# One inference step of a hybrid backbone: TensorE's order in the recurrent layer written out as a table

## The chip, the core and the metric

The kernel runs on one core of a Trainium2 chip. A core has five engines that run side by side, each with its own in-order instruction queue, and that wait for each other through semaphores: TensorE (PE in the profile, matrix products into PSUM; PEld is its weight load), VectorE (DVE), ScalarE (ACT), GpSimd (POOL) and SyncE (SP), whose queue starts most of the DMA transfers. The metric is the device time of one execution in microseconds (us), as a median of several runs. The clock named in the profile is the share of TensorE's full clock that was granted.

## The reference

Two layers run over 640 tokens of 1024 features: 512 latent tokens, which form a grid of 8 rows and 64 columns, and 128 context tokens. Layer 0 mixes tokens by neighbourhood attention, layer 1 by a recurrent unit in both directions; each is followed by a SwiGLU feed-forward layer. The change is in layer 1's mixer:

```
def _rglru_coeffs(xc, w_a, b_a, w_i, b_i, lam):
    r = sigmoid(einsum('btnk,nkj->btnj', xb, w_a) + b_a)     # xb: xc in 8 blocks of 128 features
    i = sigmoid(einsum('btnk,nkj->btnj', xb, w_i) + b_i)
    log_a = -LRU_C * r * softplus(-lam)
    return exp(log_a), sqrt(-expm1(2.0 * log_a)) * (i * xc)

def _lru_mixer(xm, h0, w_in, conv_w, conv_b, w_a, b_a, w_i, b_i, lam, w_out):
    gate, xr = split(xm @ w_in, 2, axis=-1)
    xc = _centred_depthwise_conv(xr, conv_w, conv_b)
    a_f, b_f = _rglru_coeffs(xc, w_a[0], ...)                # forward
    a_b, b_b = _rglru_coeffs(xc, w_a[1], ...)                # backward
    hs_f, hT_f = _linear_scan(a_f, b_f, h0[:, 0], reverse=False)   # h = a_t * h + b_t
    hs_b, hT_b = _linear_scan(a_b, b_b, h0[:, 1], reverse=True)
    y = (hs_f + hs_b) * gelu(gate)
    return y @ w_out, stack([hT_f, hT_b], axis=1)
```

## The kernel before

Everything is held with features on the 128 partitions, so 1024 features are eight tiles (f = 0 to 7, `KT`), and tokens along the free axis. A tile of features is also one block of the gates' weights: the eight tiles of the recurrent layer don't depend on each other until the output projection.

A plain projection of one output tile (`halves`) loads its weights, splits them into a rounded high half `whi` and a remainder `wlo`, and makes two chunks of tokens, here called a (tokens 0 to 384) and b (384 to 640). A chunk is 24 matmuls into one PSUM tile `mm`: for each of eight input tiles high times high, high times low and low times high (`some`, lines 221 to 223). In this stage the raw weights come over SyncE's queue, `whi` a second time by a DMA on GpSimd's queue (line 178), which writes and rounds it, and VectorE subtracts to get `wlo` (line 182). There are three buffers of each. `lru_xr` projects x, the input of the recurrence: in this text x3a and x3b are the two chunks of x's tile 3, and ScalarE copies them into a buffer `xr` (two of them, taken in turn). `lru_gate` projects the gate branch: chunks g3a and g3b, of which ScalarE takes the gelu.

One tile then passes four steps:

- `lru_a`: ScalarE (line 1252) and three steps of VectorE (line 1254) make the convolution `xc`. TensorE makes four gate products `gp` from `xc` (line 1264), two gates in two directions, each of 643 columns in plain 32-bit floats; ScalarE takes a tanh of each (line 1265, a sigmoid by another formula). Two PSUM buffers hold `gp`, so a product waits for the tanh of the one two before it. VectorE multiplies by `xc` (line 1266).
- `lru_b`: VectorE clamps (line 1272), ScalarE takes two exp, two tanh and one square root (lines 1276 to 1278), VectorE multiplies (lines 1279 and 1280). Switching between the functions loads a table on ScalarE (`ACT_TABLE_LOAD` in the profile).
- `lru_c`: VectorE runs four scans (line 1289), GpSimd copies the last states (line 1291), VectorE adds the directions (lines 1296 and 1297).
- `lru_d`: VectorE multiplies by the gelu (line 1301); ScalarE (line 1306) and VectorE (line 1308) split y into its two halves for the output projection.

The loop in `run` works with t = 0 to 9 and makes, for one t, `lru_a` of tile t, the projection of x's tile t + 1, `lru_b` of tile t - 1, `lru_c` of t - 2, the gate projection of t - 2 and `lru_d` of t - 2. This is the order in which the program is written. What stands in each engine's queue is then set by a planner, which orders instructions by its own estimates of durations and may mix the matmuls of several chunks and products. An order can be forced with `pin`, which lets what is issued inside it come only after a given instruction of the same engine; `chunk` takes such pins for single matmuls. Before the loop, x0a, g0a, x1a, x0b and g0b are made. After it, `project_halves` multiplies y by the output weights: three tiles run over the first six tiles of y, and wait for the last two after that.

## Time and profile before

| | us |
|---|---|
| median of 3 runs (1520.92 to 1523.51) | 1522.5 |
| the profiled execution | 1524.38 |
| its span in the trace | 1522.6 |
| TensorE busy | 1491.2 |
| VectorE busy | 1060.8 |
| ScalarE busy | 698.6 |
| the recurrent stage in the span | about 850 to 1025 |

TensorE is busy for 98% of the span. The mean granted clock is 0.991. The stage of the change is about a tenth of the span. In rows of the trace the first number is the start in us from the span's beginning, the second how long the row is busy; then follow line, engine, operation, output and inputs, shape and count; in brackets stands the idle time of the engine just ahead of the row and what ended it. Rows of one engine overlap a little, because an instruction can start before the one ahead of it has drained. A gate product shows as four matmul records, two for each call. Lines are those of the kernel before; behind the change they lie three to six higher (line 1264 becomes 1268, line 1265 becomes 1269).

### The profile page before, as it was taken

To read this page: it belongs to the slowest core of one execution; us is meant where nothing else is said; L and a number is where in the kernel's file an instruction comes from. 1 tells how busy PE (TensorE), PEld (TensorE's weight loads), DVE (VectorE), ACT (ScalarE), POOL (GpSimd) and SP (SyncE) were. 2 spreads that over 40 slices of the span, in tenths; PEclk is the share of its full clock that TensorE was granted. 3 is DMA by queue.
4 is the path that set the end of the run, shared out by engine and by line. 5 is a ranking of instruction groups with operands and counts; after the bars stand their busy time and mean duration, and the time that the engine had idled before them with its cause. 6 is when DMAs were issued, how large, how long until landed. Compare 5 with 4: busy or idle time off the path is not lost. (4 is left out here: it accounts for less than half of the span.)

```text
span 1522.6 us, 26092 instructions
## 1 busy us (share of the span) xinstructions
PE 1491.2 (98%) x10359; PEld 1443.4 (95%) x10359; DVE 1060.8 (70%) x2005; ACT 698.6 (46%) x1268; POOL 256.2 (17%) x276
## 2 busy tenths in 40 slices
PE   8999999899999999999999999999999999999997
PEld 5999999899999999999999987899999999999997
DVE  5778998669899997434443769875965656556555
ACT  4676766754332123312331478863634343425243
POOL 0112131100111110000000114220222322232211
PEclk9999999999999999999999999999999999999999
DMA  9545665335456664222222543325242231323211
GB/s 379 176 136 162 194 192 165 107 141 193 162 189 202 198 205 127 69 84 79 69 62 94 152 135 102 114 96 183 93 128 73 81 110 58 99 68 97 70 56 70
DMA packets 72330, 196.65 MB, mean 129 GB/s; under 512 B 8048, under 2 KB 24592, under 8 KB 72080
## 3 DMA queue, kind: packets, MB, share of 16 engines
q1 hardware_dynamic: 57392, 142.32, 29.0%
q0 software_dynamic: 14240, 51.98, 11.0%
q8 instruction: 81, 1.33, 0.4%
q10 hardware_dynamic: 576, 0.68, 0.1%
q14 instruction: 41, 0.34, 0.1%
HBM read 179.48 MB, written 8.92 MB: 124 GB/s over the span
## 5 line engine op out<-in xcount | busy, mean ns | idle before, releaser
L221 PE MATMUL mm<-big,whi 128*128 128x320 f32 (+3 forms) x1233 | 384.1, 313 | 5.9 <-ACT big L1306 5.3
L222 PE MATMUL mm<-big,whi 128*128 128x320 f32 (+3 forms) x1233 | 384.3, 312 | 0.5 <-DVE big L563 0.3
L223 PE MATMUL mm<-big,wlo 128*128 128x320 f32 (+3 forms) x1233 | 384.6, 313 | 0.0
L221 PEld LDWEIGHTS mm<-big,whi 128*128 128x128 f32 x1233 | 233.3, 190 | 8.3 <-ACT big L1306 6.1
L222 PEld LDWEIGHTS mm<-big,whi 128*128 128x128 f32 x1233 | 233.8, 190 | 3.0 <-DVE big L563 0.9
L223 PEld LDWEIGHTS mm<-big,wlo 128*128 128x128 f32 x1233 | 233.4, 189 | 1.5
L250 DVE SCALAR_TENSOR_TENSOR mprod<-mraw,csb 128x1024 f32<-128x1024 f32 x160 | 194.9, 1218 | 8.5 <-DMA mraw<-in_wm 8.1
L586 DVE SCALAR_TENSOR_TENSOR x<-mm,G,x 128x320 f32<-128x320 f32 (+2 forms) x192 | 78.0, 435 | 83.2 <-PE mm L223 83.1
L180 ACT CAST whi<-raw 128x1024 fp32r<-128x1024 f32 (+1 forms) x71 | 73.9, 1041 | 111.1 <-PE mm L222 65.7
L182 DVE TENSOR_TENSOR wlo<-raw,whi 128x1024 fp32r<-128x1024 f32 (+1 forms) x87 | 105.5, 1212 | 23.6 <-ACT whi L180 14.5
L221 PE MATMUL mm<-big,whx 128*128 128x320 f32 (+3 forms) x348 | 108.5, 312 | 0.0
L223 PE MATMUL mm<-big,wlx 128*128 128x320 f32 (+3 forms) x348 | 108.3, 311 | 0.0
L222 PE MATMUL mm<-big,whx 128*128 128x320 f32 (+3 forms) x348 | 108.2, 311 | 0.0
L246 POOL DMA_DIRECT2D mraw<-in_wm x80 | 43.0, 537 | 365.7 <-DVE mprod L250 274.2
L221 PE MATMUL mx<-big,whi 128*128 128x320 f32 (+3 forms) x287 | 89.6, 312 | 0.0
L223 PE MATMUL mx<-big,wlo 128*128 128x320 f32 (+3 forms) x287 | 89.1, 310 | 0.0
L222 PE MATMUL mx<-big,whi 128*128 128x320 f32 (+3 forms) x287 | 88.9, 310 | 0.0
L180 ACT CAST whx<-raw 128x1024 fp32r<-128x1024 f32 (+1 forms) x40 | 41.1, 1030 | 91.5 <-PE mm L222 51.6
L223 PE MATMUL mx<-big,wlx 128*128 128x320 f32 (+3 forms) x260 | 80.8, 311 | 0.0
L221 PE MATMUL mx<-big,whx 128*128 128x320 f32 (+3 forms) x260 | 80.8, 311 | 0.0
L222 PE MATMUL mx<-big,whx 128*128 128x320 f32 (+3 forms) x260 | 80.4, 309 | 0.0
L1306 ACT CAST whi<-raw 128x1024 fp32r<-128x1024 f32 (+1 forms) x41 | 41.4, 1009 | 70.7 <-PE mm L222 45.1
(347 smaller groups left out, 3716.2 us busy)
## 6 DMA issues: line engine op xcount, KB each, us to landing
raw<-in_gu SPq DMA_DIRECT2D x88, 512.0 KB, 3.6
mraw<-in_wm POOLq DMA_DIRECT2D x80, 512.0 KB, 3.9
raw<-in_dn SPq DMA_DIRECT2D x24, 512.0 KB, 3.5
sw<-in_wm SPq DMA_DIRECT2D x16, 512.0 KB, 10.1
raw<-in_wqk SPq DMA_DIRECT2D x16, 512.0 KB, 4.7
raw<-in_wi SPq DMA_DIRECT2D x16, 512.0 KB, 3.6
whi<-in_wi POOLq DMA_DIRECT2D x16, 512.0 KB, 3.9
raw<-in_dn SPq DMA_DIRECT2D x16, 448.0 KB, 3.3
```

The lines of the kernel that those rows point to most:

```text
L180: nc.scalar.copy(hi, raw)
L182: nc.vector.tensor_tensor(lo, raw, hi.bitcast(F32), ALU.subtract)
L221: nc.tensor.matmul(ps, hi[:, k], xhi[:, k, s], start=(k == 0), stop=False)
L222: nc.tensor.matmul(ps, hi[:, k], xlo[:, k, s], start=False, stop=False)
L223: self.done = nc.tensor.matmul(ps, lo[:, k], xhi[:, k, s], start=False, stop=(k == last)).ins
L246: nc.gpsimd.dma_start(w, self.i["wm"][l * 6 + j - 2, f])
L250: nc.vector.scalar_tensor_tensor(prod, w, 1.0, self.csb[:, s], ALU.mult, ALU.mult, accum_out=out[:, s, f:f + 1])
L586: self.nc.vector.scalar_tensor_tensor(xs, ps[:, a - t0:b - t0], G[:, s, f:f + 1], xs, ALU.mult, ALU.add)
L1306: self.nc.scalar.copy(hi, v)
```

## The change

A table `ORDER` now says which chunks of plain projections belong to each t, in order. `lru_a` gets these chunks as `steps`. Each gate product is pinned behind the last matmul of whatever chunk came before it, and after each product's tanh the next chunk is issued, its first matmul pinned behind that product. Steps that are left over follow behind `lru_a`. The order on TensorE is thus product, whole chunk, product, whole chunk, and so on; a tile has four products and three chunks (two for tile 7), so the fourth product and the next tile's first stand side by side. Nothing is computed in another way.

The chunks are also dealt out otherwise: x runs ahead of its tile as before up to x4, then x5 is spread over t = 3 and 4; of the gate branch, g1 begins at t = 1 (before, at t = 3) and ends at t = 2, g2 and g3 come at t = 3 and 4, g4 is spread over t = 5 and 6. g6 and g7 come behind the last product, as before.

```
+ORDER = ("x1b x2a x2b", "x3a x3b g1a", "x4a x4b g1b", "x5a g2a g2b", "x5b g3a g3b",
+         "x6a x6b g4a", "x7a x7b g4b", "g5a g5b", "g6a g6b", "g7a g7b")

-    def lru_a(self, f, lp):
+    def lru_a(self, f, lp, steps):
...
                 for s0, s1 in ((0, 512), (512, LW)):
-                    nc.tensor.matmul(ps[:, s0:s1], gw[:, w, d], xc[:, s0:s1], start=True, stop=True)
+                    with self.pin(self.done):
+                        gp = nc.tensor.matmul(ps[:, s0:s1], gw[:, w, d], xc[:, s0:s1], start=True, stop=True).ins
                 nc.scalar.activation(tl[:, d], ps[:, 0:LW], AF.Tanh, scale=0.5, bias=self.hb[:, c:c + 1])
+                if steps:
+                    steps.pop(0)(pins={0: gp})
...
+            chunks = {"x1b": x1[1]}
             for t in range(KT + 2):
+                steps = []
+                for chunk in ORDER[t].split():
+                    if chunk not in chunks:
+                        f = int(chunk[1])
+                        pair = self.lru_xr(f, xhi, xlo) if chunk[0] == "x" else gate(f)
+                        chunks.update({chunk[:2] + c: step for c, step in zip("ab", pair)})
+                    steps.append(chunks[chunk])
                 if t < KT:
-                    A[t] = self.lru_a(t, lp)
-                if t + 1 < KT:
-                    for step in self.lru_xr(t + 1, xhi, xlo) if t else x1[1:]:
-                        step()
+                    A[t] = self.lru_a(t, lp, steps)
+                for step in steps:
+                    step()
                 if 0 < t <= KT:
                     B[t - 1] = self.lru_b(t - 1, *A.pop(t - 1))
                 if t > 1:
                     C[t - 2] = self.lru_c(t - 2, *B.pop(t - 2))
-                if t > 2:
-                    for step in gate(t - 2):
-                        step()
                 if t > 1:
                     self.lru_d(t - 2, C.pop(t - 2), G.pop(t - 2), yhi, ylo)
```

The planner still orders ScalarE, VectorE, GpSimd and SyncE, and comes to other orders there too. The queues of all engines are word for word the same up to the first gate product. The first place is TensorE at that product. Before, `mm_9748` is x2a; x1b has been made in full ahead of it, and the first two products stand in the midst of x2a:

```order
L223 MATMUL mm_9748<-big_8886,wlo_9745 128x384
L1264 MATMUL gp_9672<-xc_9665,gw_9663 128x512
L1264 MATMUL gp_9672<-xc_9665,gw_9663 128x131
L1264 MATMUL gp_9676<-xc_9665,gw_9663 128x512
L1264 MATMUL gp_9676<-xc_9665,gw_9663 128x131
L221 MATMUL mm_9748<-big_8886,whi_9744 128x384
L222 MATMUL mm_9748<-big_8887,whi_9744 128x384
```

Now `mm_9636` is g0b and `mm_9682` is x1b:

```order
L226 MATMUL mm_9636<-big_8886,wlo_9520 128x256
L1268 MATMUL gp_9678<-xc_9671,gw_9669 128x512
L1268 MATMUL gp_9678<-xc_9671,gw_9669 128x131
L224 MATMUL mm_9682<-big_8886,whi_9525 128x256
L225 MATMUL mm_9682<-big_8887,whi_9525 128x256
L226 MATMUL mm_9682<-big_8886,wlo_9526 128x256
```

The first product has moved ahead of x1b, and x2a with it behind the second.

The second place is ScalarE around the exp of tile 0. Before, it comes between the third and the fourth tanh of tile 1 (`lt_9724`; `lt_9670` is tile 0, `xr_1598` holds x3):

```order
L1265 ACTIVATE lt_9724<-gp_9733,l_hb_2009 128x643
L1276 ACT_TABLE_LOAD
L1276 ACTIVATE lt_9802<-lt_9670,l_sm_387_2007 128x643 x2
L1277 ACTIVATE lt_9670<-lt_9670,l_sp_386_2005 128x643
L1265 ACTIVATE lt_9724<-gp_9737,l_hb_2009 128x643
L1277 ACTIVATE lt_9670<-lt_9670,l_sp_386_2005 128x643
L1244 COPY xr_1598_9503<-mm_9870 128x16x8
```

Now (tile 0 is `lt_9676`, tile 1 `lt_9797`, and `mm_9864` is g1a):

```order
L1269 ACTIVATE lt_9797<-gp_9860,l_hb_2009 128x643
L1282 ACT_TABLE_LOAD
L1282 ACTIVATE lt_9895<-lt_9676,l_sm_387_2007 128x643 x2
L1283 ACTIVATE lt_9676<-lt_9676,l_sp_386_2005 128x643 x2
L1322 COPY gl_9782<-mm_9864 128x384
L1284 ACT_TABLE_LOAD
L1284 ACTIVATE lt_9676<-lt_9676 128x1286
L1269 ACT_TABLE_LOAD
L1269 ACTIVATE lt_9797<-gp_9890,l_hb_2009 128x643
```

The exp still stands behind the third tanh of tile 1, but that tanh now belongs to a product with g1a behind it, and the square root of tile 0 comes ahead of the fourth.

The third place is VectorE at the same time. Before, with tile 2's convolution `xc_9813`, tile 3's `xc_9920` and the clamps (L1272) of tiles 1 and 2 (`lt_9723`, `lt_9818`) around tile 0's product with the square root (L1279):

```order
L1254 SCALAR_TENSOR_TENSOR xc_9813<-xr_1597_9502,cols_61,xc_9813 128x643 x2
L1272 TENSOR_SCALAR lt_9723<-lt_9723 128x1286
L1266 SCALAR_TENSOR_TENSOR lt_9724<-lt_9724,xc_9718 128x1286
L182 TENSOR_TENSOR wlo_10114<-raw_10111,whi_10113 128x1024
L1279 SCALAR_TENSOR_TENSOR lt_9670<-lt_9802,lt_9670 128x1286
L1254 SCALAR_TENSOR_TENSOR xc_9920<-xr_1598_9503,cols_61,xc_9920 128x643
L1280 TENSOR_TENSOR lt_9671<-lt_9671,lt_9670 128x1286
L1272 TENSOR_SCALAR lt_9818<-lt_9818 128x1286
```

Now (tile 2's convolution is `xc_9912`, tile 3's `xc_10053`, tile 1's clamp `lt_9796`):

```order
L1257 SCALAR_TENSOR_TENSOR xc_9912<-xr_1597_9502,cols_61,xc_9912 128x643 x3
L1278 TENSOR_SCALAR lt_9796<-lt_9796 128x1286
L185 TENSOR_TENSOR wlo_10041<-raw_10038,whi_10040 128x1024
L1285 SCALAR_TENSOR_TENSOR lt_9676<-lt_9895,lt_9676 128x1286
L1272 SCALAR_TENSOR_TENSOR lt_9797<-lt_9797,xc_9791 128x1286
L1286 TENSOR_TENSOR lt_9677<-lt_9677,lt_9676 128x1286
L1257 SCALAR_TENSOR_TENSOR xc_10053<-xr_1598_9503,cols_61,xc_10053 128x643
```

The product of tile 1's second gate (L1266, now L1272) has moved from ahead of tile 0's L1279 to behind it, and the first step of tile 3's convolution from directly behind it to two steps later.

## The prediction

> **What bounds the kernel now.** The page comes first: TensorE is nearly always busy, so the change can only act where TensorE waits or where what it waits for gets later. Behind the page I cut the recurrent stage into windows (columns: busy time of TensorE, its weight loads, VectorE, ScalarE and GpSimd; granted clock; DMA).

> ```profile
> PE 1491.2 (98%) x10359; PEld 1443.4 (95%) x10359; DVE 1060.8 (70%) x2005; ACT 698.6 (46%) x1268; POOL 256.2 (17%) x276
> ```

> ```profile
> 868.90:908.80 39.90, 39.76 (x236) 33.80 (x235) 24.56 (x24) 27.55 (x41) 2.12 (x4) 1.00 0.49 151
> 908.80:945.00 36.20, 33.88 (x199) 29.48 (x197) 35.45 (x44) 33.95 (x45) 20.57 (x10) 1.00 0.39 117
> 945.00:980.00 35.00, 33.05 (x198) 28.76 (x197) 30.62 (x37) 29.45 (x40) 7.49 (x8) 0.99 0.33 102
> 980.00:1024.70 44.70, 42.74 (x261) 39.17 (x260) 36.20 (x43) 29.08 (x39) 13.56 (x7) 0.96 0.22 75
> sum 155.80, PE 149.42 PEld 131.21 DVE 126.83 ACT 120.04 POOL 43.74; mean PE 37.35 PEld 32.80 DVE 31.71 ACT 30.01 POOL 10.94
> ```

> In this stage three engines are close to full. VectorE does 126.8 us, 15.9 us for each of the eight tiles, and is idle 15.3 us up to 908.8 but only 115.9 - 102.3 = 13.6 us in all the rest. TensorE's timeline has four waits worth naming, 5.8 us together:

> ```profile
> 918.48 1.35 PE L1264 MATMUL gp<-xc,gw 128*128 128x512 f32 x4 [1.87 <-ACT lt L1265]
> 932.24 1.35 PE L1264 MATMUL gp<-xc,gw 128*128 128x512 f32 x4 [0.46 <-ACT lt L1265]
> 979.44 4.09 PE L1264 MATMUL gp<-xc,gw 128*128 128x512 f32 x8 [1.86 <-ACT lt L1278]
> 1022.31 0.42 PE L221 MATMUL mm<-big,whi 128*128 128x320 f32 x1 [1.64 <-ACT big L1306]
> ```

> The third is put down to ScalarE, but what ended last is VectorE's third convolution step, which ends at 978.46 + 0.88 = 979.34. One tile earlier the same step ends at 945.14, just ahead of the gate product:

> ```profile
> 944.23 0.91 DVE L1254 SCALAR_TENSOR_TENSOR xc<-xr,cols,xc 128x643 f32<-128x643 f32 x1
> 945.25 2.40 PE L1264 MATMUL gp<-xc,gw 128*128 128x512 f32 x8
> 978.46 0.88 DVE L1254 SCALAR_TENSOR_TENSOR xc<-xr,cols,xc 128x643 f32<-128x643 f32 x1
> ```

> So from the fourth tile on VectorE's queue hands out the tiles, and the stage ends when y of the last two tiles leaves VectorE (the wait at 1022.31). Two of the waits are followed by some 3.4 us at a clock of 0.5 (the windows beside these rows have 0.88, 0.97 and 0.68), 1.7 us lost each time:

> ```profile
> 980.00:982.00 2.00, 2.00 (x5) 1.11 (x4) 2.00 (x2) 1.09 (x4) 0.00 (x0) 0.50 1.04 387
> 982.00:984.00 2.00, 2.00 (x8) 1.18 (x7) 1.97 (x3) 1.19 (x2) 0.00 (x0) 0.77 0.17 70
> 1024.00:1026.00 2.00, 2.00 (x10) 2.00 (x9) 2.00 (x2) 1.49 (x2) 0.00 (x0) 0.50 0.97 373
> ```

> **The change, part by part.** No product and no chunk is added or removed, so TensorE's work is unchanged; I walk the new queues with durations from these rows.

> ```profile
> 855.19 0.42 PE L221 MATMUL mm<-big,whi 128*128 128x384 f32 x1
> 859.49 0.34 PE L221 MATMUL mm<-big,whi 128*128 128x384 f32 x1
> 870.05 0.28 PE L221 MATMUL mm<-big,whi 128*128 128x256 f32 x1
> 872.89 0.34 PE L221 MATMUL mm<-big,whi 128*128 128x384 f32 x1
> 876.29 2.33 PE L1264 MATMUL gp<-xc,gw 128*128 128x512 f32 x8
> 878.37 0.42 PE L221 MATMUL mm<-big,whi 128*128 128x384 f32 x1
> 868.95 1.81 DVE L1254 SCALAR_TENSOR_TENSOR xc<-xr,cols,xc 128x643 f32<-128x643 f32 x2 [4.87 <-ACT xc L1252]
> 871.50 1.23 DVE L182 TENSOR_TENSOR wlo<-raw,whi 128x1024 fp32r<-128x1024 f32 x1 [0.74 <-DMA whi<-in_wi]
> 872.64 0.89 DVE L1254 SCALAR_TENSOR_TENSOR xc<-xr,cols,xc 128x643 f32<-128x643 f32 x1
> ```

> A 384-column chunk (a) takes 859.49 - 855.19 = 4.3 us, a 256-column one (b) 872.89 - 870.05 = 2.84, a gate product (878.37 - 876.29) / 2, with the slow first instruction behind it 1.08 us.

> (1) The first gate product moves from behind x1b and most of x2a to ahead of x1b, so it comes up at 870.05. Its input is complete at 872.64 + 0.89 = 873.5, because VectorE's queue, in the new order too, has the low half of x2's weights between the steps, and those wait for a DMA until 871.5. TensorE waits 3.5 us. Before, x1b was the cover.

> (2) From 873.55 on: four products, x1b, x2a, x2b put the end of tile 0's products at 873.55 + 4.32 + 2.84 + 4.3 + 2.84 = 887.85; three more products with x3a and x3b bring tile 1's third to 898.2. Then ScalarE's queue has: tanh until 899.2, table load, two exp of tile 0, two tanh, a copy of g1a, table load, square root.

> ```profile
> 893.45 1.28 ACT L1276 ACT_TABLE_LOAD   x1
> 894.75 1.74 ACT L1276 ACTIVATE lt<-lt,l_sm 128x643 f32<-128x643 f32 x2
> 908.20 1.73 ACT L1277 ACTIVATE lt<-lt,l_sp 128x643 f32<-128x643 f32 x2
> 915.23 0.46 ACT L1316 COPY gl<-mm 128x384 f32<-128x384 f32 x1
> 901.18 1.28 ACT L1278 ACTIVATE lt<-lt 128x1286 f32<-128x1286 f32 x1
> 902.49 1.50 DVE L1279 SCALAR_TENSOR_TENSOR lt<-lt,lt 128x1286 f32<-128x1286 f32 x1 [1.34 <-ACT lt L1278]
> ```

> That is 899.2 + 1.28 + 1.74 + 1.73 + 0.46 + 1.28 + 1.28 = 907.0, and the step of L1279 ends near 908.5 where it ended at 904.0. The exp starts at 900.5, not 894.75, because g1a and whole chunks now stand between the products of tiles 0 and 1. What has VectorE done by 908.8? In the new order 9 convolution steps, 5 weight halves, 2 clamps (L1272), one L1266, one L1279. Before, it had done 11, 5, 3, 2 and 1 of these, one L1280 and a scan.

> ```profile
> L1254 DVE SCALAR_TENSOR_TENSOR xc<-xr,cols,xc 128x643 f32<-128x643 f32 x24 | 21.2, 883 | 6.1 <-ACT xc L1252 5.9
> L1289 DVE TENSOR_TENSOR_SCAN lt<-lt,cols,lt 128x512 f32<-128x512 f32 x16 | 20.3, 1270 | 0.0
> L1266 DVE SCALAR_TENSOR_TENSOR lt<-lt,xc 128x1286 f32<-128x1286 f32 x8 | 12.0, 1498 | 11.3 <-ACT lt L1265 11.3
> L1280 DVE TENSOR_TENSOR lt<-lt,lt 128x1286 f32<-128x1286 f32 x8 | 12.0, 1494 | 0.0
> L1272 DVE TENSOR_SCALAR lt<-lt 128x1286 f32<-128x1286 f32 x8 | 6.6, 829 | 0.0
> L1301 DVE TENSOR_TENSOR lt<-lt,gl 128x640 f32<-128x640 f32 x8 | 6.5, 819 | 0.9 <-ACT gl L1320 0.9
> L1265 ACT ACTIVATE lt<-gp,l_hb 128x643 f32<-128x643 f32 x32 | 25.1, 791 | 14.2 <-PE gp L1264 13.9
> ```

> The debt is 2 x 0.88 + 0.83 + 1.50 + 1.49 + 1.2 (the scan up to 908.8) = 6.8 us, in front of a stretch in which VectorE has only 13.6 us of idle time.

> (3) From there each tile needs 15.9 us of VectorE, while TensorE's share per tile is 4 x 1.08 + 4.3 + 4.3 + 2.84 = 15.8 us, or 14.3 with one a and two b. TensorE therefore reaches each next gate product first and waits there for the convolution. Walking the queues tile by tile gives waits of about 1.6, 3.0, 4.2, 2.2 and 2.3 us ahead of tiles 3 to 7, with 3.5 at the start, 0.3 at a PSUM buffer of tile 2 and 1.2 at the end: 18.3 us against 5.8. These waits are the same delay seen from TensorE, not added to it.

> (4) ScalarE gets three table loads more (24 in the stage where before has 21), 3 x 1.28 = 3.8 us. Most lies beside the waits for VectorE. What shows is in the last two tiles, where VectorE waits for the tanh and the square root behind them; with y0's cast and the weights of x6 and g6, which are loaded into buffers that open only when an earlier chunk is through, the walk leaves VectorE some 15.6 us idle after 908.8, against 13.6: 2 us more.

> (5) The earlier gelu branches remove one wait, 0.9 us at L1301; it lies in the tail and is inside (4).

> (6) Clock: the 3.5 us wait at the start is longer than the 1.86 and 1.64 us that were followed by half clock; I add 1.7 us for it, since everything in tile 0 follows from it. Its ends are 0 and 1.7. Later waits I cost at nothing, as TensorE has 1.6 to 4.2 us of slack at the next wait; without that cover each costs up to 1.7. [...] Here a gap of 1.86 us was enough, and one of 1.87 us, at 918.48, was followed by windows at 1.00, so the measurement decides: the length alone doesn't. [...]

> Sum: 6.8 + 2 + 1.7 = 10.5 us. Bounds of the first term: 0, if the later idle time swallows it, and 15.3, all the idle time that VectorE had up to 908.8; of the second: -5, if the waits of the old order's tail are avoided, and +8 if each wait of (3) brings half clock. The profiled execution took 1524.4 us, 1.9 above the median of 1522.5; 1524.4 + 10.5 = 1534.9 there, so **1533** as a median, with a range of its own of 1526 to 1541.

> **The rivals.** *A steady alternation removes the waits* (faster). The four waits and both half-clock stretches go, -5.8 - 3.4, and the new start costs 3.5 + 1.7: -4.0, 1518.5. For it speaks that a whole chunk, at least 2.84 us, now covers each tanh (0.79) between products; against it, that the third wait was VectorE's. It decides if VectorE's idle time after 908.8 falls below 13.6 - 6.8 - 4.0 = 2.8 us, so that the convolution of tiles 3 to 7 is ready ahead of its product.

> *VectorE swallows the debt* (no change): the stage still ends with VectorE, whose work is the same 126.8 us; if 6.8 of its 13.6 us go, y ends as before, and the start wait is TensorE's alone: 1522.5.

> *Waits multiply* (slower still). The five waits of (3) each bring half clock, 5 x 1.7 = 8.5 on top: 1541.5. Also GpSimd copies the scans' last columns, and in the new order both copies of tile 0 stand ahead of the DMA of g2's weights; one copy took long while VectorE ran without a break:

> ```profile
> 911.02 12.53 POOL L1291 COPY st<-lt 128x1 f32<-128x1 f32 x1
> ```

> That would start g2's weights up to 4 us later, until VectorE itself stands still for them: part of the 8.5. [...]

> **How the numbers follow.** My forecast gets 0.54, the rivals 0.2, 0.12 and 0.14. A difference under 0.2% (3 us) is about what a measurement here can't tell from none. Faster: 0.2; same: 0.12; slower: 0.54 + 0.14 = 0.68. For eight in ten the range reaches from the fast rival's 1518.5 to just over the slow one's 1541.5: 1518 to 1543.

> **What would show it.** Right: TensorE's first gate product starts near 873.5 behind a wait of some 3.5 us, then 0.5 clock; VectorE has about 18 us done by 908.8; TensorE waits at the first product of tiles 3 to 7, ended by the convolution; the last two casts of y start near 1032 instead of 1021.5; beyond that the kernel runs as before. Wrong: the convolution is ready ahead of those products, VectorE is fuller after 908.8 than 102 of 116 us, or the last y is cast by 1024.

## The result, and the profile after

The changed kernel takes 1538.47 us (median of 4 runs, 1538.13 to 1539.35) where the kernel before takes 1523.01 in runs beside it (1520.92 to 1524.33). The ratio is 1.0101 with a 95% interval of 1.0083 to 1.012, so the change costs 15.5 us, between 12.6 and 18.3. The prediction was 1533 with a range of 1518 to 1543.

The profiled execution took 1538.3 us with a span of 1536.5, 13.9 more than the span before. Its page gives TensorE 1493.2 us busy where before it was 1491.2: the work is the same, and what grew is the time around it. Here are the windows of the recurrent stage in the changed kernel (columns as in the prediction: TensorE, weight loads, VectorE, ScalarE, GpSimd, granted clock, DMA).

```profile
PE 1493.2 (97%) x10359; PEld 1445.6 (94%) x10359; DVE 1062.6 (69%) x2005; ACT 703.1 (46%) x1271; POOL 249.9 (16%) x276
```

```profile
868.90:908.80 39.90, 36.57 (x213) 32.04 (x212) 16.82 (x17) 20.21 (x32) 2.69 (x5) 0.96 0.48 139
908.80:945.00 36.20, 32.48 (x183) 27.72 (x182) 29.18 (x34) 29.42 (x41) 8.27 (x7) 0.95 0.28 89
945.00:980.00 35.00, 30.80 (x177) 26.63 (x176) 32.78 (x37) 31.06 (x40) 6.99 (x7) 1.00 0.41 126
980.00:1024.70 44.70, 40.71 (x258) 36.98 (x257) 32.28 (x35) 37.96 (x48) 7.48 (x6) 1.00 0.23 66
1024.70:1040.00 15.30, 12.27 (x80) 11.48 (x79) 14.94 (x20) 4.85 (x9) 10.98 (x4) 1.00 0.16 52
sum 171.10, PE 152.82 PEld 134.85 DVE 126.00 ACT 123.49 POOL 36.41; mean PE 30.57 PEld 26.97 DVE 25.20 ACT 24.70 POOL 7.28
```

The stage is 171.1 us long instead of 155.8. VectorE does the same work (126.0 against 126.8) with 45.1 us of idle time instead of 29.0, and TensorE is idle 171.1 - 152.8 = 18.3 us where before it was 155.8 - 149.4 = 6.4. This is where TensorE stands, from its timeline:

```profile
875.36 1.35 PE L1268 MATMUL gp<-xc,gw 128*128 128x512 f32 x4 [3.33 <-DVE xc L1257]
922.75 1.32 PE L1268 MATMUL gp<-xc,gw 128*128 128x512 f32 x4 [1.23 <-issue]
941.04 1.90 PE L1268 MATMUL gp<-xc,gw 128*128 128x512 f32 x4 [2.46 <-ACT gl L1326]
959.33 1.10 PE L1268 MATMUL gp<-xc,gw 128*128 128x512 f32 x2 [2.23 <-issue]
977.15 1.32 PE L1268 MATMUL gp<-xc,gw 128*128 128x512 f32 x4 [1.98 <-issue]
994.26 1.32 PE L1268 MATMUL gp<-xc,gw 128*128 128x512 f32 x4 [2.65 <-ACT lt L1283]
1037.90 0.41 PE L224 MATMUL mm<-big,whi 128*128 128x320 f32 x1 [2.48 <-ACT big L1312]
```

One wait is at the start, five are ahead of the first products of tiles 3 to 7, and one is at the end, for y; the seven come to 16.4 us, and the rest of the 18.3 is short pauses. The profile names "issue" or ScalarE for the five, but what ended last is VectorE's third convolution step each time; for tile 7, at 993.28 + 0.88 = 994.16. This piece of VectorE's timeline also shows what held that step back, the low half of g6's weights, which waited for their DMA:

```profile
988.21 1.82 DVE L1257 SCALAR_TENSOR_TENSOR xc<-xr,cols,xc 128x643 f32<-128x643 f32 x2
992.14 1.23 DVE L185 TENSOR_TENSOR wlo<-raw,whi 128x1024 fp32r<-128x1024 f32 x1 [2.11 <-DMA whi<-in_wi]
993.28 0.88 DVE L1257 SCALAR_TENSOR_TENSOR xc<-xr,cols,xc 128x643 f32<-128x643 f32 x1
```

The last row starts 0.09 us before the one ahead of it ends (992.14 + 1.23 = 993.37).

The kernel before has such a wait for weights at the same place, ahead of the last convolution step of its tile 7, and a longer one, so this wait alone does not make the difference:

```profile
977.32 1.23 DVE L182 TENSOR_TENSOR wlo<-raw,whi 128x1024 fp32r<-128x1024 f32 x1 [2.91 <-DMA whi<-in_wi]
```

The stage itself begins 1.8 us later than in the profile of before, though nothing ahead of it was changed. Over all profiles of this study that start moved by up to 4.8 us from kernel to kernel, and single runs of the kernel before lay between 1516.2 and 1527.5. So from here on stages are compared by times counted from the end of tile 0's convolution (873.53 before, 875.30 after). Three marks are used: the end of the convolution of tile 3 and of tile 7, and the start of ScalarE's last cast of y. A mark comes from the one profiled execution of each kernel.

### The profile page after: what moved, and what is told of

The parts are those of the page before. It is cut to its first block, busy times and chain, and to the rows that moved or that the text cites. A ratio compares the mean times of both kernels' runs of the same rounds, so it can differ in the third digit from the quotient of the medians.

```text
span 1536.5 us, 26093 instructions
## 1 busy us (share of the span) xinstructions
PE 1493.2 (97%) x10359; PEld 1445.6 (94%) x10359; DVE 1062.6 (69%) x2005; ACT 703.1 (46%) x1271; POOL 249.9 (16%) x276
## 5 line engine op out<-in xcount | busy, mean ns | idle before, releaser
L224 PEld LDWEIGHTS mm<-big,whi 128*128 128x128 f32 x1233 | 234.5, 191 | 10.6 <-ACT big L1312 6.9
L183 ACT CAST whi<-raw 128x1024 fp32r<-128x1024 f32 (+1 forms) x71 | 73.9, 1042 | 112.1 <-PE mm L225 68.3
L249 POOL DMA_DIRECT2D mraw<-in_wm x80 | 43.1, 538 | 364.6 <-DVE mprod L253 265.4
```

What stands on the lines that cost most here:

```text
L183: nc.scalar.copy(hi, raw)
L224: nc.tensor.matmul(ps, hi[:, k], xhi[:, k, s], start=(k == 0), stop=False)
L249: nc.gpsimd.dma_start(w, self.i["wm"][l * 6 + j - 2, f])
```

## The experiments

In the table, the third column is the median less that of the kernel before in the same comparison; the last three are the marks, in us from the end of tile 0's convolution.

| kernel | what it is | us against before | tile 3 | tile 7 | last y |
|---|---|---|---|---|---|
| before | | | 38.0 | 105.8 | 148.7 |
| after | order fixed, recurrent chunks and gelus sooner | +15.5 | 47.4 | 118.9 | 164.6 |
| e3 | order fixed alone | +17.9 | 48.5 | 124.8 | 169.2 |
| e2 | order fixed, recurrent chunks sooner | +5.5 | 40.1 | 114.3 | 158.6 |
| e6 | recurrent chunks sooner alone | +7.8 | 38.0 | 114.1 | 153.8 |
| e4 | all gelus g1 to g7 sooner alone | +9.2 | 38.0 | 112.1 | 156.4 |
| e1 | after, x1b ahead of the first product | +11.6 | 43.1 | 117.1 | 164.4 |
| e5 | after, last tile's products together | +13.4 | 48.5 | 120.0 | 162.2 |
| e12 | after, each chunk ahead of its product | +13.2 | 38.2 | 119.9 | 163.5 |
| e9 | after, all products of a tile together | +33.2 | 38.0 | 139.1 | 181.3 |
| e10 | e9, gelus late, x1b first | +23.2 | 35.9 | 131.8 | 172.9 |
| e11 | e9, old dealing, x1b first | +47.6 | 53.0 | 152.2 | 193.2 |
| e8 | before, tanh for gelu | -1.9 | 38.1 | 107.5 | 147.4 |
| e7 | after, tanh for gelu | +15.3 | 47.3 | 119.8 | 164.3 |

### The parts of the change: e2, e3, e4, e6

The change does three things at once: it fixes TensorE's order, it deals the chunks of x2 to x4 and x5a to earlier turns, and it deals g1 to g3 and g4a one or two turns sooner. (Counted in turns of the program, x2 to x4 thus do not run ahead "as before" but one turn more; in TensorE's queue before, the planner had already let x2a begin ahead of tile 0's first product.) Four kernels take the parts apart, the third one only roughly: e4 moves every branch from g1 to g7 one turn sooner, while the change leaves g5 to g7 where they were.

e2, the gelu branches late again:

```diff
-ORDER = ("x1b x2a x2b", "x3a x3b g1a", "x4a x4b g1b", "x5a g2a g2b", "x5b g3a g3b",
-         "x6a x6b g4a", "x7a x7b g4b", ...
+ORDER = ("x1b x2a x2b", "x3a x3b", "x4a x4b", "x5a g1a g1b", "x5b g2a g2b",
+         "x6a x6b g3a g3b", "x7a x7b g4a g4b", ...
```

> The changed kernel, but each gelu branch is dealt as late as in the kernel before (g1 among the products of tile 3, g2 of tile 4, and so on); the recurrent chunks and the fixed alternation are kept. Theory (whole chunks among the products of tiles 0 and 1 make the debt, the gelu branches a small part: the copy of g1a, 0.46, and one table load, 1.28, ahead of the first square root): 1538.5 - 1.7 = 1537, with 1535 to 1539. Rival (the earlier gelus carry the loss through ScalarE's table loads and GpSimd's late copies): near the kernel before, 1523 to 1529.

e3, the old dealing in the fixed order:

```diff
+ORDER = ("x1b", "x2a x2b", "x3a x3b", "x4a x4b g1a g1b", "x5a x5b g2a g2b",
+         "x6a x6b g3a g3b", "x7a x7b g4a g4b", ...
```

> The fixed alternation alone: each tile's products are pinned one behind the other with chunks between, but chunks and gelu branches are dealt to the same tiles as in the kernel before, so that only x1b stands among the products of tile 0 (873.5 + 4 x 1.08 + 2.84 = 880.7 instead of 887.9 for their end). Theory (the debt comes from the chunks dealt to tiles 0 and 1): 6.8 of the 15.5 us are given back, 1538.5 - 6.8 = 1532, the start wait and its half clock stay. Rival (the alternation itself, with a product at the head of every tile, makes the loss whatever is dealt): 1537 or more.

e4, on the kernel before:

```diff
-                if t > 2:
-                    for step in gate(t - 2):
+                if 1 < t <= KT:
+                    for step in gate(t - 1):
```

> The kernel before with one edit: the gelu branch of tile t - 1 instead of t - 2 is dealt in turn t; no order of TensorE is fixed. Theory (an earlier gelu by itself saves at most the 0.9 us that VectorE waited for a gelu and costs a table load or two): 1523 within 3. Rival (the earlier gelus carry the loss): 1530 or more.

e6, on the kernel before:

```diff
+EARLY = ("x1b x2a x2b", "x3a x3b", "x4a x4b", "x5a", "x5b", "x6a x6b", "x7a x7b", "", "", "")
...
-                if t + 1 < KT:
-                    for step in self.lru_xr(t + 1, xhi, xlo) if t else x1[1:]:
-                        step()
+                for chunk in EARLY[t].split():
...
```

> The kernel before with the recurrent chunks dealt as early as in the changed kernel (x2 in turn 0, x3 in turn 1 and so on), but no order of TensorE fixed and the gelu branches where they were. Theory from the runs so far (with the order fixed, the earlier recurrent chunks gave back 10.6 us in the stage; without it, VectorE waits only 5.9 us for the convolution's first step, 4.9 of them at the start): 1521 to 1524. Rival (step 2 of the prediction: chunks of x2 and x3 dealt to tiles 0 and 1 hold their products back and make VectorE's debt): 1523.5 + 6.8 = 1530.

Measured: e2 1529.15 (ratio 1.004, 1.0025 to 1.0054), e3 1541.6 (1.0124, 1.01 to 1.0149), e4 1532.83 (1.0065, 1.0046 to 1.0085), e6 1529.22 (1.0049, 1.0031 to 1.0068). All four theories missed in size or in sign; the rivals of e3 and e4 had the number, and that of e2 nearly (it ended at 1529). Together the four give the account. Fixing the order alone costs 17.9 us. In the fixed order, the earlier recurrent chunks give 12.4 of them back (17.9 to 5.5), and the earlier gelus cost 10.0 (5.5 to 15.5). Without a fixed order the earlier recurrent chunks cost 7.8, so they only mend what the fixed order breaks: there a tile's products come at the head of its turn, and with the old dealing the next tile's input is still to be computed behind them (in e3 TensorE waits 2.43, 4.23 and 3.99 us ahead of tiles 1 to 3). The 9.2 us of e4 look like the 10.0, but they do not show that the change's earlier gelus cost as much without a fixed order: e4 moves g5 to g7 too, and its loss lies at the end, where these are missing. (In e6 the rival had the number, 1530, but not the place: tile 3's convolution is not late, tile 7's is.)

A part of these sums is the clock, which was 0.50 behind some of the waits (two stretches of 3.41 us in the changed kernel). From 6 us ahead of the origin to the last y, TensorE was idle for 6.2 us in the kernel before, 18.0 in e3, 11.4 in e2 and 18.3 in the changed kernel; half of its busy time at a clock of 0.50, my estimate of what the half clock cost it, was 1.7, 9.0, 4.4 and 3.4 us. (It is a little high: in the changed kernel matmuls of 256 columns start 0.21 us apart at a clock of 0.50, from 876.98 to 879.97, and 0.12 apart at 1.00 just behind.) So what the earlier recurrent chunks gave back in the fixed order was 6.6 us of waits and 4.6 us of clock, and what the earlier gelus cost was waits.

What e4 and e6 lose shows at one place, TensorE's wait ahead of the next projection (1.64 us in the kernel before). The first row is e4's, from its timeline:

```profile
1030.04 0.63 PE L221 MATMUL mm<-big,whi 128*128 128x320 f32 x1 [6.92 <-ACT big L1306]
```

and this is the same place in e6:

```profile
1025.65 0.63 PE L222 MATMUL mm<-big,whi 128*128 128x320 f32 x1 [7.79 <-ACT big L1307]
```

In both a stretch at a clock of 0.50 begins within this wait and lasts at least 8.4 us in e4 and 8.9 in e6, as far as the windows reach; in the kernel before it lasted 3.41.

As I read it, TensorE was full until then in the kernel before too, so a chunk that is done sooner there takes nothing out of an idle stretch; it pushes gate products behind it (the convolution of tile 7 ends 6 to 8 us later) and is missing as cover at the end.

### ScalarE's tables: e7 and e8

```diff
-            last = nc.scalar.activation(G[:, t0:NTOK], ps, AF.Gelu_apprx_tanh).ins
+            last = nc.scalar.activation(G[:, t0:NTOK], ps, AF.Tanh).ins
...
```

> The changed kernel with the gelus replaced by tanh (a function that shares the table of exp; the output is another, the instruction and its size are the same), so that 7 of the 24 table loads of the stage go. To be compared with the kernel before with the same replacement. Theory (ScalarE's table loads carry what the earlier gelus cost): it is some 9 us slower than its counterpart instead of 15.5, at about 1529. Rival (TensorE's order carries all of it): it keeps 14 to 16 us to its counterpart.

> The kernel before with the gelus replaced by tanh, as the counterpart of the run above: 6 of the 21 table loads of the stage go. Both theories: a gain of at most 6 x 1.28 = 7.7 us and probably 1 to 3, since the waits for the square root take only 3.1 us in the kernel before: 1520 to 1523.

Measured: e7 1536.78, e8 1519.56, a difference of 17.2 us, against 15.5 with the gelus. The gelus' table loads (7 of the 24 in the changed kernel, 6 of the 21 before, 1.28 us each) do not carry the loss, though VectorE's waits for the square root suggested it. e2 says the same, since it has as many table loads as the changed kernel.

### Start and end: e1 and e5

e1:

```diff
-            for step in (x1[0], x0[1], g0[1]):
+            for step in (x1[0], x0[1], g0[1], x1[1]):
...
-ORDER = ("x1b x2a x2b", ...
+ORDER = ("x2a x2b", ...
```

> The changed kernel, but x1b stands ahead of the first gate product, as a cover for the wait for tile 0's convolution; everything else of the order is kept. Theory (the start wait and the half clock behind it are part of the debt that VectorE never gets back): the wait of 3.3 us shrinks below 1 us, the half-clock stretch behind it goes, the last product of tile 0 is through 2.8 + 1.7 = 4.5 us sooner, and all of that reaches the end: 1538.5 - 4.5 = 1534. Rival (the start is TensorE's alone, VectorE's queue makes the time later): the wait goes, the waits ahead of tiles 3 to 7 grow by as much, 1538.5 within 1.5.

e5:

```diff
-                    A[t] = self.lru_a(t, lp, steps)
+                    A[t] = self.lru_a(t, lp, steps if t < KT - 1 else [])
```

> The changed kernel, but the four gate products of the last tile (tile 7) are not followed by chunks: g5a and g5b come behind all four. Theory (in the last tile a whole chunk between the products delays the last tanh: 18.7 us from the end of its convolution to the last tanh, against 14.7 in the kernel before, and nothing behind it can take that back): 1538.5 - 4 = 1534.5. Rival (the tail waits for ScalarE's tables and VectorE's queue, whatever TensorE does): within 1.5 of 1538.5.

e1 took 1535.23 (1.0082, 1.0059 to 1.0104), e5 1534.86 (1.0086, 1.0068 to 1.0104). In e1 the start wait fell from 3.33 to 0.56 us and the convolution of tile 3 came 4.3 us sooner, as the theory has it. But of the 4.3 us only 1.8 were left at tile 7 and 0.2 at the last y: by these marks the rival is right, while the median lies 3.2 us below the changed kernel's, in the sense of the theory. The intervals of the two ratios overlap, so the size stays open. The profile does not show the rival's cause either, waits that grow by as much: between the convolutions of tiles 3 and 7 TensorE is idle for 10.3 us in e1 and 9.3 in the changed kernel. What differs more is the clock, which by the same estimate costs 3.4 us there in e1 and 1.7 in the changed kernel, and from tile 7 to the last y 2.7 and nothing; these 4.4 us are about what was given back. The longest wait of e1 is at tile 7 (GpSimd, VectorE, TensorE):

```profile
980.47 2.78 POOL L1296 COPY st<-lt 128x1 f32<-128x1 f32 x1 [0.46 <-DVE lt L1294]
983.19 0.53 POOL L180 DMA_DIRECT2D whi<-in_wi  x1
987.03 1.23 DVE L184 TENSOR_TENSOR wlo<-raw,whi 128x1024 fp32r<-128x1024 f32 x1 [2.91 <-DMA whi<-in_wi]
989.16 1.93 PE L1267 MATMUL gp<-xc,gw 128*128 128x512 f32 x4 [3.92 <-ACT lt L1268]
```

The DMA of g6's weights starts the moment GpSimd is through with its copy of a scan's last column, VectorE waits 2.91 us for the weights with a convolution step queued behind, and TensorE 3.92 us for that. In the changed kernel the same two waits are 2.11 and 2.65 us.

e5 moved the end by 2.4 us in the profile (162.2 against 164.6), its convolution of tile 7 being 1.1 us later; its median is 3.6 below the changed kernel's, again with overlapping intervals. The theory had 4.

### Where the products stand: e9 to e12

After the first runs I held that the chunks between a tile's products were the mechanism: they put the last tanh 17 to 30 us behind the convolution, where before it comes 11 to 19 behind. e9 puts the four products together, with the dealing kept:

```diff
-                if steps:
-                    steps.pop(0)(pins={0: gp})
+        if steps:
+            steps.pop(0)(pins={0: gp})
```

> The changed kernel with the same chunks dealt to the same tiles and the order still fixed, but a tile's four gate products stand together and its chunks behind them. Theory (every whole chunk between two products makes the tile's last tanh later, 17 to 29 us after the convolution against 11 to 18 in the kernel before, and VectorE's queue, which has the steps that wait for that tanh ahead of the next convolution, hands the delay on): the last tanh comes 7 to 9 us after the convolution, the waits ahead of tiles 3 to 7 mostly go, the start wait stays: 1523 to 1531. Rival (a product at the head of each tile's turn, with nothing ahead of it, makes the loss): 1536 or more.

e10 is e9 with x1b as in e1 and the gelu branches as in e2:

```diff
+ORDER = ("x2a x2b", "x3a x3b", "x4a x4b", "x5a g1a g1b", "x5b g2a g2b", ...
```

> The run above with two edits more: x1b ahead of the first product and the gelu branches as late as in the kernel before. Theory (the spread is the mechanism, the start wait and the early gelu branches add to it): 1519 to 1525, so about as fast as the kernel before or faster. Rival (chunks done early leave TensorE without cover at the end of the stage, as where only the recurrent chunks were dealt sooner): 1529 or more, with a wait of several us ahead of the next projection.

e11 is e9 with x1b as in e1 and the dealing of e3:

```diff
+ORDER = ("", "x2a x2b", "x3a x3b", "x4a x4b g1a g1b", ...
```

> Products together in a fixed order, chunks and gelu branches dealt as in the kernel before, x1b ahead of the first product. Theory (the spread alone is the mechanism): 1519 to 1526. Rival (the next tile's recurrent chunks, now behind all four products, come too late for its convolution): waits of 2 to 4 us ahead of the products of tiles 1 to 3 and 1530 or more, as with the fixed alternation of the same chunks (1541.6), from which only the spread is taken.

Measured: e9 1556.24 (1.0218, 1.0204 to 1.0232), e10 1546.25 (1.0152, 1.0138 to 1.0166), e11 1570.67 (1.0319, 1.0299 to 1.0339). The theory fell: in e9 tile 0's last tanh came 5.6 us after its convolution, the convolution of tile 3 as early as in the kernel before (38.0), and the kernel was 17.8 us slower still than the changed one. Its largest wait:

```profile
962.40 7.48 PE L1268 MATMUL gp<-xc,gw 128*128 128x512 f32 x16 [11.12 <-issue]
```

All the chunks of that turn stand behind this product, and in the fixed order TensorE may take none of them. The times of e10 and e11 pass the bounds of their rivals (1529 and 1530 or more). The wait that e10's rival named did not come: TensorE waits 0.58 us ahead of the next projection. In e11 the waits came where its rival had them, but at 11.62 and 10.13 us ahead of tiles 2 and 3 instead of 2 to 4.

The last kernel keeps the alternation and moves each chunk from behind its product to ahead of it:

```diff
+                if steps:
+                    steps.pop(0)(**({"pins": {0: self.gp}} if hasattr(self, "gp") else {}))
...
-                        gp = nc.tensor.matmul(...
+                        self.gp = nc.tensor.matmul(...
...
-                if steps:
-                    steps.pop(0)(pins={0: gp})
```

> The changed kernel with the same chunks dealt to the same tiles and the same fixed alternation, but each chunk stands ahead of its product instead of behind it: chunk, product, chunk, product, chunk, product, product. So the first product of every tile (tile 0's too) has a whole chunk ahead of it as cover. Theory (TensorE waits because the fixed order brings the first product of a tile right behind the last one of the tile before, with work behind it that it may not take): the 3.3 us at the start shrink below 1, the five waits ahead of tiles 3 to 7, 10.5 us together, fall to some 3, and the time is 1538.5 - 10 = 1528, with 1524 to 1532. Rival (the convolution of the next tile hangs on the tanhs of this one through VectorE's queue, so that a later product brings a later convolution): the waits stay at 8 us or more in all and the time is 1535 or more.

It took 1535.29 (1.0082, 1.0067 to 1.0098): the rival. The waits at the start and ahead of tile 3 are gone and tile 3's convolution is as early as before, yet the time comes back behind it. The longest wait is at tile 7, and its cause stands on GpSimd's queue once more, here with g7's weights (GpSimd, VectorE and TensorE of e12):

```profile
979.63 5.51 POOL L1297 COPY st<-lt 128x1 f32<-128x1 f32 x1 [0.47 <-DVE lt L1295]
985.08 0.53 POOL L181 DMA_DIRECT2D whi<-in_wi  x1
989.98 1.23 DVE L185 TENSOR_TENSOR wlo<-raw,whi 128x1024 fp32r<-128x1024 f32 x1 [4.88 <-issue]
992.10 2.48 PE L1270 MATMUL gp<-xc,gw 128*128 128x512 f32 x4 [6.72 <-issue]
```

So I read the stage as a loop through four in-order queues: products, tanhs, VectorE's steps and the weights' DMAs each wait for the others. The delay taken out at the start of e12 is taken again at later tiles, and most of that in e1, there with the clock's help. In every kernel with the fixed alternation and the early gelus (after, e1, e5, e7, e12) tile 7's convolution ends at 117 to 120, whatever tile 3's did (38 to 48). What pins it there was not tried alone; the weights' DMAs behind GpSimd's copies are a candidate, seen ahead of tile 7 in after, e1 and e12 (2.1, 2.9 and 4.9 us of VectorE's time), but at most a part of it, since the kernel before has 2.91 us there too and ends that convolution at 105.8.

No kernel of the study was faster than the kernel before, apart from e8, which computes another function.

## Why the prediction was right, and where not

The forecast was slower by 10.5 us in the profiled execution. Found: 13.9 us of span, of which 1.8 lie ahead of the stage, so 12.1; by the medians 15.5. By the medians the kernel is 5.5 us above the forecast of 1533 and 3.0 below the 1541.5 of the rival that waits multiply, so the number was nearer to that rival's.

Step (1), the start wait: 3.5 forecast, 3.33 measured, in front of a product at 875.36 (873.5 plus the late start of 1.8). Right, by its mechanism too: e1 shows that x1b is the cover that went missing.

Step (6), the clock: half speed followed that wait, as forecast (see the last section), and once more behind the wait of 2.46 us, 3.4 us lost in all, by the estimate of half the busy time. But the kernel before has two such stretches as well, one ahead of its last y (from 979.51) and one right behind it (from 1023.88), and a third at 1098.98, where the changed kernel has none in the 100 us behind its last y. Up to there the term is -1.7, not 1.7: the sum charged the new stretch and did not credit the old ones that went with the old order.

Step (2), the debt: the exp of tile 0 was forecast at 900.5 without the late start and the half clock, 904.0 with both.

```profile
903.83 1.74 ACT L1282 ACTIVATE lt<-lt,l_sm 128x643 f32<-128x643 f32 x2
```

The convolution of tile 3 is 9.4 us later than before (47.4 against 38.0), against 6.8 + 1.7 = 8.5 forecast. Right in size. Its attribution was only half right (it names g1a, but its walk to the exp holds only chunks of x): with the same chunks of x2 and x3 among the products but the gelu chunks away (e2), it is 2.1 us later. So the chunks of g1 among the products of tiles 1 and 2 carry the other 7.3: the last tanh of tile 2 comes 52.5 us after the origin, in e2 44.0.

Step (3) said that the waits ahead of tiles 3 to 7 are that debt seen from TensorE, not added to it. The waits came, at the places named: 3.33 against 3.5 at the start, 1.23, 2.46, 2.23, 1.98 and 2.65 ahead of tiles 3 to 7 against 1.6, 3.0, 4.2, 2.2 and 2.3, and 2.48 against 1.2 at the end. They come to 16.4 us, not 18.3; that TensorE's whole idle time is 18.3 as well is a coincidence, since it counts the short pauses too. But that they are only the debt is refuted by e12 and e9, in which tile 3's convolution has no delay and the waits come anyway: the fixed order makes its own.

Step (4) failed in size. It allowed 2 us more for all that comes after the debt; measured are 3.7 us between the convolutions of tiles 3 and 7 (13.1 later against 9.4), and 2.8 from there to the last y (15.9 against 13.1), 6.5 together. VectorE's idle time after 908.8, forecast at 15.6 us, was 22.0, and the last two casts of y, forecast near 1032, started at 1037.12 and 1039.93. From tile 7's convolution to the last y it takes 42.9 us in the kernel before, 45.7 in the changed kernel and 42.2 in e5. So the whole chunks between the products of the last tile, which the sum had not costed, carry these 2.8 us, as far as single profiles tell. Without the gelus' table loads the difference is no smaller (44.5 in e7 against 39.9 in e8).

So the stage ends 15.9 us later, 5.4 more than the sum, and the kernel only 12.1. Of the 3.8 us that came back, 3.4 are the two half-speed stretches behind the last y of the kernel before, which the changed kernel does not have. That the 10.5 came so near to 12.1 is therefore luck.

Step (5) costed the earlier gelu branches as a gain of at most 0.9 us. They cost 10.0 within the change (e4's 9.2 are for a wider move). It looked at the gelu, when what is moved is its two chunks of TensorE's work, which stand ahead of later products.

The rivals: that a steady alternation removes the waits is refuted by the timeline, with waits of 16.4 us where 5.8 were. That VectorE swallows the debt is refuted for the change as a whole; for the start wait alone e1 leaves it open. That waits multiply was wrong on the clock, since one of the five waits was followed by half speed, and right on GpSimd: VectorE waited for g2's weights, whose DMA stood behind both copies of tile 0.

```profile
919.13 2.76 POOL L1297 COPY st<-lt 128x1 f32<-128x1 f32 x1 [0.47 <-DVE lt L1295]
921.84 1.05 POOL L181 DMA_DIRECT2D whi<-in_wi  x2
925.68 1.23 DVE L185 TENSOR_TENSOR wlo<-raw,whi 128x1024 fp32r<-128x1024 f32 x1 [2.29 <-issue]
```

The rival's up to 4 us for these weights was an estimate; what VectorE waited is 2.29 us. Why one copy of a column takes 12.53 us (before, at 911.02) and another 1.00 (before, at 909.39), with VectorE busy beside both, was not shown.

## What to carry to other kernels

Where several in-order queues wait for each other, a fixed order of the busiest engine costs whatever that engine may not take while it waits (here 17.9 us, e3); ask of every pinned instruction what stands behind it and could have run. Work that was dealt sooner on an engine that was already full was no gain here (7.8 us lost in e6, 9.2 in e4): by my reading it pushes what others wait for, and it is missing as cover at the end. A change of several parts is costed part by part on the kernel before and on top of the other parts, since here one part cost 7.8 us alone and gave 12.4 back beside another.

## What the runs showed of the hardware

```profile
873.36:876.78 3.42, 1.42 (x6) 0.94 (x7) 2.54 (x3) 0.04 (x1) 0.00 (x0) 1.00 0.88 192
876.78:880.19 3.41, 3.41 (x19) 3.41 (x18) 0.62 (x1) 0.76 (x1) 0.00 (x0) 0.50 0.72 255
938.22:941.64 3.42, 0.96 (x5) 0.56 (x4) 3.42 (x7) 2.78 (x4) 2.37 (x2) 1.00 0.34 77
941.64:945.05 3.41, 3.41 (x15) 2.90 (x14) 2.27 (x4) 1.88 (x3) 1.13 (x2) 0.50 0.30 101
...
989.42:992.83 3.41, 2.19 (x14) 1.52 (x12) 1.30 (x2) 3.39 (x6) 0.53 (x1) 1.00 0.70 183
992.83:996.25 3.42, 1.99 (x9) 1.54 (x10) 3.42 (x4) 3.39 (x6) 0.00 (x0) 1.00 0.87 268
996.25:999.66 3.41, 3.41 (x22) 3.41 (x21) 3.41 (x5) 3.38 (x4) 0.00 (x0) 1.00 0.38 82
```

The wait of 2.65 us ahead of tile 7 is cut in two by the edge at 992.83, 1.2 us of idle time in one slot and 1.4 in the next, and nothing follows; the 2.46 us ahead of tile 4 lie in one slot, and the next runs at half speed. In this stage of the six profiles every slot at full speed with 1.99 us idle or more was followed by half speed, none with 1.61 or less was, and between 1.79 and 1.95 both occurred. The two waits that the prediction set side by side fit: the 1.86 us at 979.44 in the kernel before lay in one slot, the 1.87 us at 918.48 were cut into 1.44 and 0.43 by the edge at 918.05. The count is not to be carried to other work: just ahead of the stage the slot from 849.48 to 852.89 of the changed kernel, with some 128x1 matmuls in it, had 0.88 us idle and was followed by half speed. So the prediction's "the length alone doesn't decide" was right: in this stage the place of the slot's edge decided beside it. Each kernel has one profile, so whether one and the same wait meets the edge in the same place in every execution, no run here shows.
